# Retention offsets on GpSimd, and the outputs of a state space moved one to two steps back, split in two and spread over two PSUM banks

## The chip, the cores and the metric

The kernel runs on one core of one Trainium2 chip. The metric is the device time of one execution in microseconds (us), the median over several runs. Engines are named as the profile names them: PE is TensorE (matmuls; PEld is its weight loads), DVE is VectorE, ACT is ScalarE, POOL is GpSimd, SP is SyncE, which issues DMAs.

## The reference

A trunk of two layers runs over two groups of 1024 tokens of width 1024, each with its own conditioning vector. Layer 0 projects the normed tokens once and feeds two branches with the result: bidirectional retention with four heads of 128, and a state-space model (S5) with 32 groups of 16 channels and 64 complex states. Both are gated, concatenated and projected back. Layer 1 is neighbourhood attention. Cut to what the change touches:

```python
def _retention(q, k, v):            # chunks of 128 tokens, n = 8 chunks, 4 heads
    s = jnp.einsum('bnihd,bnjhd->bnhij', qc, kc) * intra
    o = jnp.einsum('bnhij,bnjhe->bnihe', s, vc)
    ...
    o = (o + jnp.einsum('bnihd,nbhde->bnihe', qc * q_fwd, st_f)
         + jnp.einsum('bnihd,nbhde->bnihe', qc * q_bwd, st_b))

def _head_norm(o):
    mu = jnp.mean(of, axis=-1, keepdims=True)
    var = jnp.mean(jnp.square(of - mu), axis=-1, keepdims=True)
    return (of - mu) * lax.rsqrt(var + EPS)

def _s5_scan(u, ...):               # x[t] = abar * x[t-1] + bbar * u[t], then a real part
    _, _, x_re, x_im = lax.associative_scan(_cplx_combine, elems, reverse=reverse, axis=1)
    return einsum(x_re, c_re) - einsum(x_im, c_im)
```

The S5 output of both directions goes through a tanh GELU and then a gated linear unit.

## The kernel before

All large products are split in three fp32r matmuls (high by high, low by high, high by low parts, "h_hi", "h_lo", "wh", "wl"), 128x512 each. TensorE is fed in **units**: one unit is about one half of a dense block, 24 such matmuls into bank d. After each, `unit()` (L183) steps every background task once, in the order of its list, and a task emits its next few instructions there up to its `yield`. Three tasks matter in layer 0: `s5` (the state space, four units per pair of groups, 16 pairs), `mod_blocks` (the modulation of the next layer, L341, alternating between two kinds of step) and `ret_mix` (retention of one head and one token group, L969). From the end of the first loads on, TensorE's instructions stay in the order in which the program emits them (L132, L137). DVE, ACT and POOL are ordered by a scheduler, which is why a shift in the program moves instructions there too.

PSUM has eight banks. In layer 0, bank d has two buffers and a, b, c, z, y, e have one each (`pst`, L164): the first matmul into a bank waits until every reader of its last content is done, and all later TensorE instructions wait with it.

What each part of `s5` does, for a pair `pi` of groups g = 0, 1:

- `s5_begin`: POOL builds the output tables car and cai (L685 products, sum L703, difference L706) and the input table ep (L685, sum L712), through two scratch tiles ta, tb; u is loaded.
- `s5_tables`: DVE builds the rotation tables cos and sn (four L685, then L730, L733, L734), through the same scratch tiles ta, tb.
- `s5_matrices`: TensorE transposes ep into bank e ("pev", printed pse<-ident,E), ACT copies it to em (L202); TensorE makes kernel taps in bank z ("kv"), ACT and DVE copy them (kf, k0: L202, L763, L764), and DMAs put them into mt.
- `s5_states(g)`: TensorE em by u into bank z; DVE rotates (L787, L788), POOL adds (L789), DVE scans four times (L792) and rotates back (L793, L794), POOL adds (L795).
- `s5_place(g)`: ACT copies the states, shifted, into xs (L202).
- `s5_out(g)`: six matmuls into bank y (mt by u, car and cai by the states), ACT squares (L813), DVE (L814), ACT tanh (L815), DVE (L817), store. Bank y is free after L817.

`mod_blocks` uses bank e too: in one step eight products and a copy by ACT (L202), in the next a product with the selector ("p2", printed pse<-sel), which DVE reads (L371). It does so while pairs 0 to 4 run.

In `ret_mix`, `outputs` makes the product in bank b, DVE takes statistics (L1028, L1029), L206 (DVE) and L207 (POOL, a power) make the reciprocal root brs, and DVE the offset bnb = -mean * brs (L1031). A unit later `normal` lets ACT apply both (L1037) into a tile `on`, `finish` transposes it, DVE gates it in place (L1045), and a DMA stores it to oD. Each head does this twice, first for half 1, then for half 0. Region A8 of the fixed memory map holds one sd tile (scores) and one on tile.

Of the kernel before, what the change touches and what calls it, by code (L numbers as in the profile page):

```python
# [17 lines left out]
ADD, SUB, MUL = ALU.add, ALU.subtract, ALU.mult  # L18

P = 128  # L20
# [18 lines left out]
def _parts(text):  # L39
# [28 lines left out]
MAP_L0.update(_parts("A5 gsg 1024 gsg 1024 gsg 1024 gsg 1024; A10 gth 1024 gth 1024 gbo 2048"))  # L68
MAP_L0.update(
    cosT=_fulls("A0"), sinT=_fulls("A1"), kT=_fulls("A11 A12"), qT=_fulls("A13"), ga=_fulls("A14"),  # L70
# [47 lines left out]
class Trunk:  # L118
# [573 lines left out]
    def s5_begin(self, pi):  # L692

        nc, G = self.nc, self.nc.gpsimd
        pp = self.t([P, PK], "pp")
        self.load(pp, self.ppD[pi])
        (bre, bim, cre, cim), (pwr, pwi, pwn), _ = self.s5_fields(pp)
        car = self.t([P, 2, 9, 16], "car")
        cai = self.t([P, 2, 9, 16], "cai")
        ta, tb = (self.t([P, 2, 9, 16], x) for x in ("ta", "tb"))  # L700
        self.outer(G, ta, pwr, cre)
        self.outer(G, tb, pwn, cim)
        G.tensor_tensor(car, ta, tb, ADD)  # L703
        self.outer(G, ta, pwn, cre)
        self.outer(G, tb, pwr, cim)
        G.tensor_tensor(cai, ta, tb, SUB)  # L706
        ep = self.t([P, 2, 2, 8, 16], "ep")
        for r, (x, y, op) in enumerate(((bre, bim, SUB), (bim, bre, ADD))):
            ta, tb = (self.t([P, 2, 8, 16], x) for x in ("ta", "tb"))
            self.outer(G, ta, pwr[:, :, 7::-1], x)  # L710
            self.outer(G, tb, pwi[:, :, 7::-1], y)
            G.tensor_tensor(ep[:, :, r], ta, tb, op)  # L712
        u = self.t([P, 2, 2, P], "u")
        for g in range(2):
            gi = 2 * pi + g
            for s in range(2):
                self.load(u[:, g, s], self.uD[s][gi * 16:gi * 16 + 16].rearrange("i t c -> t i c"))
        return dict(pi=pi, pp=pp, car=car, cai=cai, ep=ep, u=u, x=[None, None])

    def s5_tables(self, st):  # L720

        Vv = self.nc.vector
        cF, sF, cA, sA = self.s5_fields(st["pp"])[2]
        cos = self.t([P, 2, 8, 16], "cos")
        sn = self.t([P, 2, 2, P], "sn")
        ta, tb = (self.t([P, 2, 8, 16], x) for x in ("ta", "tb"))
        fl = lambda z: z.rearrange("p g a b -> p g (a b)")
        self.outer(Vv, ta, cA, cF)
        self.outer(Vv, tb, sA, sF)
        Vv.tensor_tensor(cos, ta, tb, SUB)  # L730
        self.outer(Vv, ta, sA, cF)
        self.outer(Vv, tb, cA, sF)
        Vv.tensor_tensor(sn[:, 0], fl(ta), fl(tb), ADD)  # L733
        Vv.tensor_scalar(sn[:, 1], sn[:, 0], -1.0, None, MUL)  # L734
        st.update(cos=cos, sn=sn)
        for d in range(2):
            rows = slice(64 * d, 64 * d + 64)
            self.copy_a(self.bm[rows, :, :, 32 * d:32 * d + 16],
                        st["pp"][rows, 0:64].rearrange("p (r g i) -> p g r i", r=2, g=2))

    def s5_matrices(self, st):

        nc, Vv, pi = self.nc, self.nc.vector, st["pi"]
        pev = self.pst("e").rearrange("p (g r x) -> p g r x", g=2, r=2)
        for g in range(2):
            for r in range(2):
                self.tr(pev[:, g, r], st["ep"][:, g, r].rearrange("p t i -> p (t i)"), self.ident)
        em = self.t([P, 2, 2, P], "em")
        self.copy_a(em, pev)
        kv = self.pst("z")[:, 0:144]  # L750
        for r, c in enumerate(("car", "cai")):
            for g in range(2):
                self.mm(kv[64 * g:64 * g + 48], self.bm[:, g, r], st[c][:, g].rearrange("p m i -> p (m i)"),
                        start=(r == 0), stop=(r == 1))
        kf = self.t([16, 2, 240], "kf")
        dd = self.t([16, 2, 16], "dd")
        k0 = self.ring(self.sml, [16, 2, 16], "k0")
        self.load(dd, self.I["dd"][:, 2 * pi:2 * pi + 2])
        for g in range(2):
            self.copy_a(kf[:, g, 0:128], kv[64 * g + 32:64 * g + 48, 16:144])  # L760
            self.copy_a(kf[:, g, 128:240], kv[64 * g:64 * g + 16, 16:128])
            self.copy_a(k0[:, g], kv[64 * g:64 * g + 16, 0:16])
        Vv.tensor_tensor(k0, k0, dd, ADD)  # L763
        Vv.tensor_tensor(kf[:, :, 112:128], k0, kf[:, :, 112:128], ADD)  # L764
        mt = self.t([P, 2, P], "mt")
        for s in range(8):
            self.load(mt[16 * s:16 * s + 16], kf[:, :, (7 - s) * 16:(7 - s) * 16 + 128])
        st.update(em=em, mt=mt)
# [34 lines left out]

    def s5_out(self, st, g):
        nc, Vv = self.nc, self.nc.vector
        x, gi = self.xs[g], 2 * st["pi"] + g
        ys = self.pst("y")[:, 0:256]
        yv = ys.rearrange("p (s c) -> p s c", s=2)
        self.mm(yv, st["mt"][:, g], st["u"][:, g], start=True, stop=False)
        self.mm(yv, st["car"][:, g, 1:9].rearrange("p m i -> p (m i)"), x[:, 0:2], start=False, stop=False)  # L810
        self.mm(yv, st["cai"][:, g, 1:9].rearrange("p m i -> p (m i)"), x[:, 2:4], start=False, stop=True)
        y2 = self.t([P, 256], "y2")
        nc.scalar.activation(y2, ys, AF.Square, scale=0.044715 ** 0.5)  # L813
        Vv.scalar_tensor_tensor(y2, y2, 1.0, ys, ADD, MUL)  # L814
        nc.scalar.activation(y2, y2, AF.Tanh, scale=G0)  # L815
        g2 = self.t([P, 2, P], "g2")
        Vv.scalar_tensor_tensor(g2.rearrange("p s c -> p (s c)"), y2, 1.0, ys, ADD, MUL)  # L817
        for s in range(2):
            self.store(self.yD[s][gi * 16:gi * 16 + 16].rearrange("i t c -> t i c"), g2[:, s])

    def s5(self, tables):

        for o, z in tables:
            self.store(self.ppD.rearrange("a p x -> p a x")[:, :, o:o + z.shape[2]], z)
        self.xs = [self.t([P, 4, P], f"xs{i}") for i in range(2)]
        self.bm = self.t([P, 2, 2, 48], "bm")
        for x in self.xs + [self.bm]:
            self.nc.gpsimd.memset(x, 0.0)
        yield
        st = self.s5_begin(0)  # L830
        yield
        self.s5_tables(st)
        yield
        self.s5_matrices(st)
        yield
        for pi in range(16):
            self.s5_states(st, 0)
            if pi:
                self.s5_out(last, 1)
            nx = self.s5_begin(pi + 1) if pi < 15 else None  # L840
            yield
            self.s5_states(st, 1)
            yield
            self.s5_place(st, 0)
            if nx:
                self.s5_tables(nx)
            yield
            self.s5_place(st, 1)
            if nx:
                self.s5_matrices(nx)  # L850
            self.s5_out(st, 0)
            last, st = st, nx
            yield
        self.s5_out(last, 1)

    def ub(self, s):
        def item(m):
# [111 lines left out]
    def ret_mix(self, s, h, r):  # L969

        nc = self.nc
# [41 lines left out]
        def outputs(j, m, bank):  # L1013
            qf, qb, sd = m
            po3 = self.pst(bank).rearrange("p (c e) -> p c e", c=4)
            for c in range(4):
                ch = 4 * j + c
                f, b = ch > 0, ch < 7
                self.mm(po3[:, c], sd[:, c], vn(ch), start=True, stop=False)
                if f:  # L1020
                    self.mm(po3[:, c], qf[:, c], stf[:, ch], start=False, stop=not b)
                if b:
                    self.mm(po3[:, c], qb[:, c], stb[:, ch], start=False, stop=True)
            st = self.ring(self.sml, [P, 4, 6], "bst")
            mv = self.ring(self.sml, [P, 4, 2], "bmv")
            rs, nb = (self.ring(self.sml, [P, 4], x) for x in ("brs", "bnb"))
            for c in range(4):
                Vv.bn_stats(st[:, c], po3[:, c])  # L1028
                Vv.bn_aggr(mv[:, c], st[:, c])  # L1029
            self.rsqrt(rs, mv[:, :, 1], 4, 1.0, EPS)  # L1030
            Vv.scalar_tensor_tensor(nb, mv[:, :, 0], -1.0, rs, MUL, MUL)  # L1031
            return po3, rs, nb

        def normal(po3, rs, nb):
            on = self.t([P, 4, P], "on")
            for c in range(4):
                nc.scalar.activation(on[:, c], po3[:, c], AF.Identity, bias=nb[:, c:c + 1], scale=rs[:, c:c + 1])  # L1037
            return on
# [513 lines left out]
```

## Time and profile before

| what | value |
|---|---|
| time, median of 3 runs | 2241.8 us (2239.88 to 2252.94) |
| the profiled execution's own time | 2248.46 us |
| its span | 2246.5 us |
| mean granted TensorE clock | 0.989 of full speed |
| PE busy | 2176.6 us, 97% of the span |
| DVE, ACT, POOL busy | 1315.4, 957.3, 746.6 us |
| chain that ended last: PE, DVE, DMA, POOL, ACT | 82%, 6%, 4%, 3%, 2% |

A busy engine is only a limit where the others wait for it. TensorE is busy nearly throughout; its few idle stretches, what ended them, and the stretches at a lower granted clock are what can be won or lost. In rows of the timeline the first two numbers are start and duration in us; x4 counts instructions shown in one row; a bracket at the end gives the idle time of the engine ahead of the instruction and what ended it.

### The profile page before, as it was taken

The page shows a single profiled execution, that of the slowest core. Times are in us where ns is not written, and L with a number is a line of the kernel's source. Part 1 is how long each engine was busy: PE and PEld are TensorE (multiplying, and loading weights), DVE is VectorE, ACT ScalarE, POOL GpSimd, SP SyncE. Part 2 cuts the span into 40 slices and gives each one's busy share as a digit, 9 for nine tenths or more (in the row PEclk, how much of TensorE's full clock was granted, in tenths as well). Part 3 has the DMA queues.
Part 4 walks back from the last instruction along what each step waited for, and adds up shares of the span by engine and source line. Part 5 has one row for each costly group of instructions (what it writes and reads, how often), then busy time and mean ns, then how long its engine had stood idle before and what let it go on. Part 6 is the DMA issues. An engine that isn't in the chain of part 4 may idle for free.

```text
span 2246.5 us, 35103 instructions
## 1 busy us (share of the span) xinstructions
PE 2176.6 (97%) x13248; PEld 1832.5 (82%) x13248; DVE 1315.4 (59%) x2885; ACT 957.3 (43%) x2098; POOL 746.6 (33%) x640
## 2 busy tenths in 40 slices
PE   6899999998999999999999999999999999999998
PEld 4667778886877888888889898888888898987886
DVE  4935768788787556566434545456555555557322
ACT  4533434435444444343334444446444444345211
POOL 2344446457465121366621111113111212113333
PEclk9999999999999999999999999999999999999999
DMA  9894222224211335534531112125111111115454
GB/s 327 264 267 127 78 83 52 67 72 129 65 58 47 95 127 178 180 132 163 166 80 44 51 46 64 46 57 111 55 50 49 51 55 55 55 38 160 113 137 125
DMA packets 296480, 231.12 MB, mean 103 GB/s; under 512 B 58488, under 2 KB 267768, under 8 KB 296312
## 3 DMA queue, kind: packets, MB, share of 16 engines
q1 hardware_dynamic: 292856, 220.51, 33.2%
q10 hardware_dynamic: 3456, 8.39, 1.1%
q8 instruction: 104, 1.70, 0.3%
q14 instruction: 64, 0.52, 0.1%
HBM read 169.92 MB, written 56.84 MB: 101 GB/s over the span
## 4 chain that ended last, share of the span: by engine, by line
PE 82%; DVE 6%; DMA 4%; POOL 3%; ACT 2%; issue 2%; SPq 0%; ACTq 0%; DVEq 0%; POOLq 0%
PE psd L131 61%; PE psc L131 5%; PE psa L131 5%; PE psb L136 4%; PE psz L131 2%; PE psy L131 2%; PE psb L131 2%; DVE E L792 1%; DMA oD<-A 1%; PE psa L136 1%; DMA wr<-in_w_in_ab 1%; PE pse L131 1%; DMA wm<-in_w_mod 0%; DMA wr<-in_w_out_ab 0%; PE psc L136 0%
## 5 line engine op out<-in xcount | busy, mean ns | idle before, releaser
L131 PE MATMUL psd<-h_hi,wh 128*128 128x512 f32 x1392 | 555.2, 399 | 8.1 <-DVE A L876 5.4
L131 PE MATMUL psd<-h_lo,wh 128*128 128x512 f32 x1392 | 547.6, 393 | 3.2 <-POOL h_lo L476 3.1
L131 PE MATMUL psd<-h_hi,wl 128*128 128x512 f32 x1392 | 545.6, 392 | 0.0
L131 PEld LDWEIGHTS psd<-h_hi,wh 128*128 128x128 f32 x1392 | 263.4, 189 | 65.2 <-DVE A L876 5.8
L131 PEld LDWEIGHTS psd<-h_lo,wh 128*128 128x128 f32 x1392 | 263.3, 189 | 58.1 <-POOL h_lo L476 5.2
L131 PEld LDWEIGHTS psd<-h_hi,wl 128*128 128x128 f32 x1392 | 263.0, 189 | 56.0 <-issue 0.4
L131 PE MATMUL psd<-wh,h_hi 128*128 128x256 f32 (+1 forms) x960 | 279.8, 304 | 3.7 <-DVE A L943 2.7
L131 PE MATMUL psd<-wl,h_hi 128*128 128x256 f32 (+1 forms) x864 | 251.7, 291 | 0.1
L202 ACT ACTIVATE wh<-wr 128x1024 fp32r<-128x1024 f32 x118 | 124.8, 1058 | 241.7 <-PE psd L131 137.0
L213 POOL TENSOR_TENSOR wl<-wr,wh 128x1024 fp32r<-128x1024 f32 x51 | 126.5, 2480 | 264.1 <-ACT wh L202 230.4
L131 PE MATMUL psd<-wh,h_lo 128*128 128x256 f32 x768 | 214.2, 279 | 0.0
L131 PEld LDWEIGHTS psd<-wh,h_hi 128*128 128x128 f32 x960 | 181.4, 189 | 12.7 <-DVE A L943 3.1
L131 PEld LDWEIGHTS psd<-wl,h_hi 128*128 128x128 f32 x864 | 163.2, 189 | 3.9 <-POOL wl L213 0.5
L131 PEld LDWEIGHTS psd<-wh,h_lo 128*128 128x128 f32 x768 | 145.4, 189 | 0.3
L1233 POOL TENSOR_TENSOR A<-A,A 128x256 f32<-128x256 f32 (+1 forms) x80 | 56.5, 727 | 264.5 <-DVE nm L1251 260.1
L213 DVE TENSOR_TENSOR wl<-wr,wh 128x1024 fp32r<-128x1024 f32 x67 | 89.5, 1336 | 72.8 <-ACT wh L202 72.8
L1253 ACT ACTIVATE E<-E,nm 128x368 f32<-128x368 f32 (+1 forms) x172 | 98.0, 571 | 52.8 <-DVE nm L1251 52.5
L395 DVE TENSOR_TENSOR rs<-ss 128x1 f32<-128x1 f32 x64 | 41.2, 643 | 119.0 <-ACT h_lo L1150 56.4
L1271 DVE COPY A<-psb 128x384 f32<-128x384 f32 x64 | 33.5, 523 | 122.6 <-PE psb L136 121.3
L685 POOL TENSOR_TENSOR A<-A 128x288 f32<-128x288 f32 (+1 forms) x128 | 93.7, 752 | 31.1 <-DVE E L733 19.5
L131 PE MATMUL psd<-ow,oh 128*128 128x512 f32 x320 | 100.4, 392 | 1.0 <-ACT oh L202 1.0
L1233 POOL TENSOR_TENSOR A<-A 128x368 f32<-128x368 f32 x16 | 13.9, 892 | 254.2 <-DVE nm L1251 253.7
(352 smaller groups left out, 4405.0 us busy)
## 6 DMA issues: line engine op xcount, KB each, us to landing
wr<-in_w_in_c SPq DMA_DIRECT2D x64, 512.0 KB
wr<-in_w_in_ab SPq DMA_DIRECT2D x48, 512.0 KB
wr<-oD SPq DMA_DIRECT2D x32, 512.0 KB
wn<-in_w_mod SPq DMA_DIRECT2D x24, 512.0 KB
wm<-in_w_mod SPq DMA_DIRECT2D x8, 1024.0 KB
ox<-in_x SPq DMA_DIRECT2D x16, 512.0 KB
x1D<-ox SPq DMA_DIRECT2D x16, 512.0 KB
oD<-E SPq DMA_DIRECT2D x32, 256.0 KB
```

Of the source, the lines that this page charges most:

```text
L131: i = self.nc.tensor.matmul(*a, **k)
L136: i = self.nc.tensor.transpose(*a, **k)
L202: self.nc.scalar.activation(dst, src, AF.Copy, scale=scale)
L213: e.tensor_tensor(lo, raw, hi.bitcast(F32), SUB)
L395: self.nc.vector.tensor_tensor(rs, ss[:, 0:1], ss[:, 1:2], ADD)
L685: eng.tensor_tensor(dst, x.unsqueeze(3).to_broadcast(sh), y.unsqueeze(2).to_broadcast(sh), op)
L792: Vv.tensor_tensor_scan(t1[:, q], r8, t1[:, q], 0.0, MUL, ADD)
L1233: self.nc.gpsimd.tensor_tensor(b, raw[a][:, c0:c0 + n], mask, ADD)
L1253: nc.scalar.activation(sn, sn, AF.Exp, bias=nm, scale=-1.0, accum_out=su)
L1271: self.nc.vector.tensor_copy(pt, pp)
```

## The change

1. In `outputs`, DVE writes bnb = -mean straight after the statistics, and after the power POOL multiplies it by brs (16 places). Before, DVE did both in one instruction after the power.
2. The `on` tile is gone: `normal` writes over the sd tile that the scores came in, and region A8 holds two sd tiles in turn.
3. In `s5` the pieces stand in other units. Per pair, units 1 to 4:

| unit | before | after |
|---|---|---|
| 1 | states(st,0); out(last,1); begin(next) | place(last,1); states(st,0); out(last,0) |
| 2 | states(st,1) | states(st,1); gelu(last,0); out(last,1); begin(next) |
| 3 | place(st,0); tables(next) | gelu(last,1); tables(next) |
| 4 | place(st,1); matrices(next); out(st,0) | place(st,0); matrices(next) |

`s5_out` is cut in two: matmuls, square and L814 stay; tanh and the rest are `s5_gelu`. Output 0 goes into bank y, output 1 into bank e. The two copies into bm move from the tables to the matrices.

```diff
-    "A7 qf 2048 qb 2048; A8 sd 2048 on 2048; A9 vfb 2048 th 2048; A10 rt1 2048 rt2 2048")
+    "A7 qf 2048 qb 2048; A8 sd 2048 sd 2048; A9 vfb 2048 th 2048; A10 rt1 2048 rt2 2048")
...
     def s5_out(self, st, g):
         nc, Vv = self.nc, self.nc.vector
-        x, gi = self.xs[g], 2 * st["pi"] + g
-        ys = self.pst("y")[:, 0:256]
+        x = self.xs[g]
+        ys = self.pst("ye"[g])[:, 0:256]
...
         nc.scalar.activation(y2, ys, AF.Square, scale=0.044715 ** 0.5)
         Vv.scalar_tensor_tensor(y2, y2, 1.0, ys, ADD, MUL)
+        st["y"][g] = ys, y2
+
+    def s5_gelu(self, st, g):
+        nc, Vv, gi = self.nc, self.nc.vector, 2 * st["pi"] + g
+        ys, y2 = st["y"][g]
         nc.scalar.activation(y2, y2, AF.Tanh, scale=G0)
...
+        last = None
         for pi in range(16):
+            if last:
+                self.s5_place(last, 1)
             self.s5_states(st, 0)
-            if pi:
+            if last:
+                self.s5_out(last, 0)
+            yield
+            self.s5_states(st, 1)
+            if last:
+                self.s5_gelu(last, 0)
                 self.s5_out(last, 1)
             nx = self.s5_begin(pi + 1) if pi < 15 else None
             yield
-            self.s5_states(st, 1)
+            if last:
+                self.s5_gelu(last, 1)
+            if nx:
+                self.s5_tables(nx)
             yield
             self.s5_place(st, 0)
             if nx:
-                self.s5_tables(nx)
-            yield
-            self.s5_place(st, 1)
-            if nx:
                 self.s5_matrices(nx)
-            self.s5_out(st, 0)
             last, st = st, nx
             yield
-        self.s5_out(last, 1)
+        self.s5_place(last, 1)
+        for g in range(2):
+            self.s5_out(last, g)
+            yield
+            self.s5_gelu(last, g)
...
+            Vv.tensor_scalar(nb, mv[:, :, 0], -1.0, None, MUL)
             self.rsqrt(rs, mv[:, :, 1], 4, 1.0, EPS)
-            Vv.scalar_tensor_tensor(nb, mv[:, :, 0], -1.0, rs, MUL, MUL)
-            return po3, rs, nb
-
-        def normal(po3, rs, nb):
-            on = self.t([P, 4, P], "on")
+            G.tensor_tensor(nb, nb, rs, MUL)
+            return po3, rs, nb, sd
+
+        def normal(po3, rs, nb, on):
```

In the lines of the changed kernel all numbers behind the changed loop are 15 higher (L1037 is L1052, L943 is L958, L876 is L891); tanh is L820, the last DVE step of an output L822, and POOL's new multiply L1047.

**TensorE, unit 2 of pair 2.** psz<-E are the states of group 1, pse<-sel is p2 of `mod_blocks`. Before:

```order
L131 MATMUL psd_2313<-h_hi,wl_1755 128x512
L131 MATMUL psz_2346<-E_193_1408 64x256 [waits DMAHW4_49,DMAHW5_49,DVE_49,PE_49]
L131 MATMUL psz_2346<-E_193_1408 64x256 x3
L131 MATMUL pse_2361<-sel,A_191_1393 128x2 [waits Activation_49]
L131 MATMUL psb_2365<-vn_237_1809,A_257_2084 128x128
```

After:

```order
L131 MATMUL psd_2282<-h_hi,wl_1751 128x512
L131 MATMUL psz_2315<-E_193_1408 64x256 [waits DMAHW5_49,DMAHW6_49,DVE_49,PE_49]
L131 MATMUL psz_2315<-E_193_1408 64x256 x3
L131 MATMUL pse_2334<-E_193_1408,E_198_1452 128x256 [waits Activation_49]
L131 MATMUL pse_2334<-E_183_1343,A_192_1395 128x256
L131 MATMUL pse_2334<-E_183_1343,A_184_1344 128x256
L131 MATMUL pse_2357<-sel,A_191_1393 128x2 [waits DVE_49,PE_49]
L131 MATMUL psb_2361<-vn_236_1797,A_257_2080 128x128
```

The six matmuls of output 1 (three rows, each for two parts) now stand in bank e directly ahead of p2, which goes into bank e as well and now waits for DVE. The same stands in units 2 of pairs 1, 3 and 4.

**DVE, the same unit.** L787, L788 rotate the states, L213 makes a low weight part, L876 or L891 the gate of retention, L814 and L822 belong to output 1, L792 are the scans, L371 reads p2. Before:

```order
L787 TENSOR_TENSOR E_217_1593<-psz_2346,E_198_1452 128x512
L788 TENSOR_TENSOR E_217_1593<-psz_2346,E_183_1343 128x512
L371 TENSOR_TENSOR mods<-pse_2361,bmod 128x2
L213 TENSOR_TENSOR wl_2340<-wr_2338,wh_2339 128x1024
L876 SCALAR_TENSOR_TENSOR ga_2243<-A_259_2093,psd_2313 128x512
```

After:

```order
L787 TENSOR_TENSOR E_217_1593<-psz_2315,E_198_1452 128x512
L788 TENSOR_TENSOR E_217_1593<-psz_2315,E_183_1343 128x512
L213 TENSOR_TENSOR wl_2309<-wr_2307,wh_2308 128x1024
L891 SCALAR_TENSOR_TENSOR ga_2231<-A_259_2089,psd_2282 128x512
L814 SCALAR_TENSOR_TENSOR A_184_1344<-A_184_1344,pse_2334 128x256
L792 SCALAR_TENSOR_TENSOR E_217_1593<-A_191_1393,E_217_1593 128x128 x4
L822 SCALAR_TENSOR_TENSOR E_198_1452<-A_184_1344,pse_2334 128x256
L793 TENSOR_TENSOR E_217_1593<-E_217_1593,E_183_1343 128x512
L371 TENSOR_TENSOR mods<-pse_2357,bmod 128x2
```

L822, the last reader of bank e, stands behind L213, the gate, L814 and the four scans. In pair 1 it stands directly behind L814; in pair 3 behind L213, L958, L959, L814, four L792 and L960; in pair 4 behind L958, L959, L814 and L960.

**POOL, units 2 to 4 of pair 2, after the change.** L712 are the two sums of ep, L795 the last step of the states, L1019 and L1020 belong to retention:

```order
L795 TENSOR_TENSOR E_217_1593<-E_217_1593 128x512
L712 TENSOR_TENSOR E_183_1343<-A_191_1393,A_192_1395 128x2x128
L1020 TENSOR_TENSOR A_256_2079<-qT_1699,A_210_1540 128x512
L685 TENSOR_TENSOR A_191_1393<-A_191_1393 128x256
L685 TENSOR_TENSOR A_192_1395<-A_191_1393 128x256
L1019 TENSOR_TENSOR A_256_2079<-qT_1699,A_210_1540 128x512
L207 TENSOR_TENSOR brs_2375<-brs_2375,mhalf 128x4
L712 TENSOR_TENSOR E_183_1343<-A_191_1393,A_192_1395 128x2x128
L1047 TENSOR_TENSOR bnb_2376<-bnb_2376,brs_2375 128x4
```

The second L712, on which pev waits, stands behind L795; before the change both L712 stood ahead of the L795 of group 1.

## Rows read from the trace of the kernel before

**Rows 1.** The page, part 1: busy time of each engine.
```profile
PE 2176.6 (97%) x13248; PEld 1832.5 (82%) x13248; DVE 1315.4 (59%) x2885; ACT 957.3 (43%) x2098; POOL 746.6 (33%) x640
```

**Rows 2.** Windows: length, busy of PE, PEld, DVE, ACT, POOL, then PEclk.
```profile
250.00:850.00 600.00, 569.88 (x3310) 475.93 (x3309) 441.42 (x861) 258.94 (x565) 295.76 (x273) 0.97 0.28 81
```

**Rows 3.** Waits of PE, 230 to 830 us: total, times, longest.
```profile
PE psy L131 <- DVE E L817: 6.4, 4, 2.8
PE psa L131 <- DVE qT L945: 5.9, 2, 3.5
PE psd L131 <- DVE A L876: 5.4, 1, 5.4
PE psz L131 <- ACT k L202: 3.9, 3, 2.3
PE pse L131 <- ACT E L202: 2.9, 1, 2.9
PE psd L131 <- DVE A L943: 2.7, 1, 2.7
```

**Rows 4.** Windows that begin at the end of four of these waits.
```profile
280.00:287.00 7.00, 7.00 (x33) 6.82 (x34) 3.49 (x12) 2.25 (x10) 0.00 (x0) 0.57 0.41 122
312.00:316.00 4.00, 3.83 (x16) 3.23 (x17) 4.00 (x8) 1.30 (x4) 3.90 (x3) 0.66 0.55 167
371.00:375.00 4.00, 3.11 (x10) 2.50 (x11) 1.62 (x3) 1.80 (x6) 0.91 (x2) 0.57 0.09 21
531.00:538.00 7.00, 6.53 (x21) 5.24 (x22) 6.44 (x12) 3.11 (x4) 2.27 (x3) 0.70 0.75 218
```

**Rows 5.** Timeline: two outputs, from their matmuls to DVE's last step.
```profile
215.39 1.03 PE L131 MATMUL psy<-E,A 128*128 128x256 f32 x4
...
217.78 0.42 DVE L817 SCALAR_TENSOR_TENSOR E<-A,psy 128x256 f32<-128x256 f32 x1 [0.48 <-ACT A L815]
...
332.02 0.70 PE L131 MATMUL psy<-E,E 128*128 128x256 f32 x2
...
332.56 1.03 PE L131 MATMUL psy<-E,A 128*128 128x256 f32 x4
...
336.25 3.92 DVE L792 TENSOR_TENSOR_SCAN E<-A,E 128x128 f32<-128x128 f32 x4
340.08 0.39 DVE L817 SCALAR_TENSOR_TENSOR E<-A,psy 128x256 f32<-128x256 f32 x1
```

**Rows 6.** DVE by line and shape, 230 to 830 us: busy, mean ns.
```profile
L792 DVE TENSOR_TENSOR_SCAN E<-A,E 128x128 f32<-128x128 f32 x115 | 74.1, 703 | 11.9 <-POOL E L789 11.9
L685 DVE TENSOR_TENSOR A<-A 128x256 f32<-128x256 f32 x54 | 37.7, 736 | 6.9 <-POOL E L712 6.7
L213 DVE TENSOR_TENSOR wl<-wr,wh 128x1024 fp32r<-128x1024 f32 x25 | 35.5, 1422 | 18.1 <-ACT wh L202 18.1
L944 DVE TENSOR_TENSOR A<-A,sinT 128x512 f32<-128x512 f32 x28 | 24.1, 860 | 0.0
...
L943 DVE TENSOR_TENSOR A<-psd,cosT 128x512 f32<-128x512 f32 x28 | 19.2, 685 | 8.7 <-ACT A L202 8.6
...
L945 DVE TENSOR_TENSOR kT<-A 128x512 f32<-128x512 f32 x14 | 11.7, 837 | 0.1
```

**Rows 7.** Timeline near 565 us: POOL's sum of ep and of states, pev.
```profile
563.85 0.74 POOL L712 TENSOR_TENSOR E<-A,A 128x256 f32<-128x256 f32 x1
...
567.39 0.60 PE L136 MATMUL pse<-ident,E 128*128 128x128 f32 x4
...
570.06 1.50 POOL L795 TENSOR_TENSOR E<-E 128x512 f32<-128x512 f32 x1 [2.97 <-DVE E L794]
```

**Rows 8.** Chain of waits, 350 to 375 us: the store of half 1.
```profile
356.13 7.86 DMA oD<-A
```

**Rows 9.** Lines L1031 and L207: instructions, shortest, median, longest ns.
```profile
L1031 DVE SCALAR_TENSOR_TENSOR bnb<-bmv,brs x16: 149/164/2330, 275.4 to 848.1; 128x4 f32<-128x4 f32 x16
...
L207 POOL TENSOR_TENSOR brs<-brs,mhalf x16: 1007/1018/1461, 272.3 to 846.8; 128x4 f32<-128x4 f32 x16
```

More of the change, by code (lines that the diff above doesn't have):

```diff
@@ L717, in s5_begin @@
                 self.load(u[:, g, s], self.uD[s][gi * 16:gi * 16 + 16].rearrange("i t c -> t i c"))
-        return dict(pi=pi, pp=pp, car=car, cai=cai, ep=ep, u=u, x=[None, None])
+        return dict(pi=pi, pp=pp, car=car, cai=cai, ep=ep, u=u, x=[None, None], y=[None, None])
     def s5_tables(self, st):
@@ L735, in s5_tables, with s5_matrices @@
         st.update(cos=cos, sn=sn)
+    def s5_matrices(self, st):
+        nc, Vv, pi = self.nc, self.nc.vector, st["pi"]
         for d in range(2):
@@ L739, in s5_tables @@
                         st["pp"][rows, 0:64].rearrange("p (r g i) -> p g r i", r=2, g=2))
-    def s5_matrices(self, st):
-        nc, Vv, pi = self.nc, self.nc.vector, st["pi"]
         pev = self.pst("e").rearrange("p (g r x) -> p g r x", g=2, r=2)
```

## The prediction

> **What bounds the kernel now.** I read the busy times first: TensorE works through 97% of the span and no other engine through more than 59% [rows 1], so a piece of work moved off DVE, ACT or POOL is worth nothing by itself. Only what makes TensorE wait, or run at the lower clock, can be won or lost. So I looked next at the stretch that the change touches, 250 to 850 us. There TensorE is idle for 600 - 569.88 = 30.1 us, and the mean granted clock is 0.97, which is 0.03 * 600 = 18 us of lost clock [rows 2]. Together 48 us, 2.1% of the time: more than that no reordering of this stretch can give.
>
> Then the table of TensorE's waits, to see who ends the 30 us. The reader is to see six entries: bank y waits for the last DVE step of an output (6.4 us, four times), the scores of retention for the rotary step (5.9), bank z for ACT's copies of the taps (3.9), p2 in bank e for ACT's copy of em (2.9), one dense half for DVE's rotary step (2.7) and one for the gate (5.4) [rows 3]. Last, the clock behind these waits. Four windows that begin where a wait ends show it at 0.57, 0.66, 0.57 and 0.70, part of the window at the half level of 1.2 GHz [rows 4]. (1 - 0.57) * 7 = 3.0 us, 0.34 * 4 = 1.4, 0.43 * 4 = 1.7 and 0.30 * 7 = 2.1 us are lost there: 2.0 us on the mean. A wait of 2 us or more so costs nearly twice its length.
>
> **What can be won.** Bank y took two outputs per pair, close behind each other; it takes one now, with four units between them, so the 6.4 us of bank y go. The copies of the taps are late for two reasons: an output stood behind them in the same unit, which is moved, and once `normal` waited for the store of half 1, 7.86 us long [rows 8], which the second sd tile ends; the 3.9 us go. The tables move behind the states of group 1 and mostly behind the rotary steps on DVE; four L685 of 0.736 us are 2.9 us of DVE that the rotary step no longer waits for [rows 6], which covers 5.9 us in two places and 2.7 in one to the greater part. I take 6.4 + 5.9 + 3.9 + 2.7 = 18.9 us. Five of these waits (those near 312, 371, 572, 668 and 726 us) are 2 us or longer; with 1.55 us each, the mean of the second and third window of rows 4, the clock gives 7.8 us. The 2.9 us in front of p2 come from a chain on ACT that begins with the offsets of retention; after the change the offset stands on POOL behind one L712, so it comes hardly earlier. I count half of 2.9 + 3.0 us, 3.0. The 5.4 us behind the gate hang on a load of weights and activations that the change leaves where it is: nothing. **Gain 18.9 + 7.8 + 3.0 = 29.7 us** (bounds: 15 if half of the waits only move; 40 with all of p2 and the gate's 5.4 + 2.1).
>
> **What it costs: bank e.** In units 2 of pairs 1 to 4 the output into bank e stands directly ahead of p2 in the same bank, and p2 must now wait for DVE's L822. There is no work between them that would cover it, and all dense work is queued behind p2. The trace gives the time from the end of an output's matmuls to the end of its last DVE step: 215.39 + 1.03 = 216.42 to 218.20, so 1.8 us with DVE free, and 333.59 to 340.47, so 6.9 us with scans between [rows 5]. Which it is, DVE's order decides; L787 and L788, two steps of about 0.69 us, fit beside the 1.6 us of the matmuls themselves. Pair 1: nothing between, 1.8 us. Pair 2: 1.42 (L213) + 0.69 (gate, priced as L943) + 0.41 + 4 * 0.70 (scans) + 0.41 = 5.7. Pair 3: 1.42 + 0.69 + 0.86 + 0.41 + 2.81 + 0.84 + 0.41 = 7.4. Pair 4: 0.69 + 0.86 + 0.41 + 0.84 + 0.41 = 3.2 [rows 5, 6]. That is 18.1 us (bounds 4 * 1.8 = 7.1 and 4 * 7.4 = 29.7). Behind each the clock falls: 4 * 2.0 = 8.0 (0, if waits of 1.8 us leave it alone, to 4 * 3.0 = 12). **26.1 us.**
>
> The Trainium skill bears on this (TensorE: Matmul & The Clock Gate, section "A second HAM failure mode: psum-queue depth-cycling"): a kernel that cycled through its PSUM banks left TensorE idle for short times between its groups so often that the clock kept falling and rising, although each matmul looked no longer at full clock. The windows behind the waits agree with that, 0.57 to 0.70 [rows 4]; by the rule alone the shortest of the four waits would pay as the others do, 8.0 us as in the sum, and the short waits that go would have given more.
>
> **The em copy.** In unit 4 the six matmuls of an output, 332.02 to 333.59 or 1.6 us [rows 5], stood between the transposes of ep and p2, while ACT copied em out of the same bank. They are gone, so p2 waits sooner at its four places: between 0 and 4 * 1.6 = 6.3 us. **I take 3.**
>
> **pev.** POOL's second L712 stands behind L795 now. Near 565 us L795 ended at 571.56; with 0.74 for L712 the transposes could start at 572.3, against 567.39 before, 4.9 us later [rows 7]. But the 2.9 us of L685 and the waits of the tables for POOL leave the way ahead of these states, so about 2 remain, and at most pairs pev comes later in the unit. I take 3 us of idle in all and one fall of 1.6, **5 us** (bounds 0, and five pairs at 4.9 + 1.6 = 32).
>
> **The rest, at nothing.** POOL's multiply of 128x4 has no row of its own: between DVE's 0.16 us for the same numbers and the power's 1.02 [rows 9]; it is nearest to the power, one POOL instruction of the same shape, so 1.0, sixteen times. It replaces a wait of bnb in DVE's queue, and `normal` follows a unit later, which hides it; without that cover it would delay ACT and the transposes behind it by 1 us, 16 in all. The additional DVE step costs the 0.16 that the old one did. The pieces moved to other units take ACT, DVE and their stores with them in equal numbers; ACT is busy for 258.94 of 600 us [rows 2], and that hides them. The last two outputs end up to two units later, ahead of the gated linear unit; if the retention work does not cover that, it is one wait of at most 6.9 us.
>
> On the multiply the Trainium skill speaks against the change (GPSIMD Engine Reference, section "Engine selection"): elementwise work with two inputs belongs on VectorE, since GpSimd takes about twice as long. No row here shows this very product on both engines; by the page it would be about 0.3 us, an estimate, and at either figure the sum stays.
>
> **Sum.** Cost 26.1 + 3 + 5 = 34.1, gain 29.7, net +4.4 on the profiled execution's 2248.46, so 2252.9. That execution lies 6.7 us above the median of the runs, 2241.8; so **2246 us**.
>
> **The rivals.**
> *Short waits on bank e.* DVE reaches L822 at all four places as fast as it did at 217.78 [rows 5]: 7.1 us and no fall of the clock, 19 less than in the sum: 2227. For it speaks that TensorE, once held, lets DVE catch up; against it, that the order puts the scans and the rotary steps ahead of L822. If the gate's wait went too (7.5), it would be 2220.
> *pev waits for POOL*, the one that ends slower. If L794 comes no earlier, five of the pairs wait 4.9 us at the transposes and pay 1.6 for the clock: 32.5 in place of 5: 2246 + 27.5 = 2274. It decides from the point where L712 ends more than 3 us behind the last dense matmul of unit 3 in most pairs. For it: the chain L794, L795, L712 is serial and stands at 571.56 + 0.74 against 567.39 [rows 7]. Against: the tables' DVE work leaves its front.
> *Stalls only move.* Half of the gain comes back elsewhere, since DVE has the same work (441 of 600 us) [rows 2]: 2246 + 15 = 2261.
>
> **How the numbers follow.** I give my forecast (2232 to 2260) 0.52, the short waits 0.16, the POOL wait 0.18, the moved stalls 0.14. About 1% (22 us) is what a measurement of this kernel tells from no change: faster means below 2219, slower above 2264. Below 2219 needs the short waits and more: 0.09. Above 2264 lie nearly all of the POOL wait and a part of the moved stalls: 0.24. The rest, 0.67, is within 1%. The range from 2226 (short waits) to 2272 (just under the full POOL wait) leaves out about 0.07 below and 0.12 above.
>
> **What would show it.** In the waits of the changed kernel: the entries of bank y and of k gone; a new one, bank e for DVE's L822, four times, some 18 us, beginning in units 2 of pairs 1 to 4, with a clock near 0.6 behind each; the scores without a wait for the rotary step; the gate's 5.4 us still there. If bank e totals under 9 us, the term for DVE's order is wrong; if bank e waits for POOL's L712 by more than 8 us, the term for pev is. If the waits for the rotary step or for k remain, the gain was overrated, and the prediction fails on the slow side.

## The result and the profile after

The changed kernel takes 2262.2 us (median of 4 runs, 2260.5 to 2266.6), the kernel before 2242.9 on the same occasions (2239.9 to 2252.9). The ratio is 1.0085, 95% interval 1.0070 to 1.0099: 19 us slower, 0.85%. Forecast were 2246 us and a range of 2226 to 2272. The time lies in the range, 2 us above the 2232 to 2260 that stood for the forecast's own account and 2 us below the 2264 from which the prediction would call it slower. The sign of the sum was right (+4.4), its size was not.

TensorE's waits in the changed kernel, 200 to 870 us; the columns are those of [rows 3]:

```profile
PE pse L131 <- DVE E L822: 23.8, 4, 7.8
PE pse L136 <- POOL E L712: 16.5, 9, 6.1
PE pse L131 <- ACT E L202: 4.4, 4, 1.7
```

Five of the six entries of [rows 3] are gone. The sixth, p2 behind the em copy, has grown from 2.9 us in one place to 4.4 in four. Two new entries stand beside it, of bank e like it: p2 behind the output of group 1, and the transposes of ep behind POOL's second sum. The stretch as a whole, first of the kernel before, then of the changed one (columns as in [rows 2]):

```profile
200.00:870.00 670.00, 639.67 (x3809) 537.09 (x3808) 486.90 (x949) 293.19 (x646) 314.96 (x295) 0.97 0.28 82
```

```profile
200.00:870.00 670.00, 625.35 (x3685) 523.29 (x3684) 453.89 (x925) 287.46 (x631) 309.80 (x309) 0.95 0.27 78
```

TensorE is idle for 670 - 625.35 = 44.7 us where it was 30.3. That is 14.3 of the 18.4 us by which the profiled span grew (2264.9 us against 2246.5). The rest, some 4 us, is put down to the clock, whose mean falls from 0.97 to 0.95. Where the idle time lies, from the timeline of TensorE in the changed kernel:

```profile
203.22 0.38 PE L131 MATMUL pse<-sel,A 128*128 128x2 f32 x2 [1.70 <-ACT E L202]
...
223.35 0.35 PE L131 MATMUL pse<-sel,A 128*128 128x2 f32 x2 [1.92 <-DVE E L822]
...
266.13 0.56 PE L131 MATMUL pse<-sel,A 128*128 128x2 f32 x2 [6.41 <-DVE E L822]
...
286.94 0.38 PE L131 MATMUL pse<-sel,A 128*128 128x2 f32 x2 [1.70 <-ACT E L202]
...
317.23 0.56 PE L131 MATMUL pse<-sel,A 128*128 128x2 f32 x2 [7.79 <-DVE E L822]
...
365.46 0.56 PE L131 MATMUL pse<-sel,A 128*128 128x2 f32 x2 [7.64 <-DVE E L822]
...
558.51 0.90 PE L136 MATMUL pse<-ident,E 128*128 128x128 f32 x3 [6.08 <-POOL E L712]
...
593.92 0.90 PE L136 MATMUL pse<-ident,E 128*128 128x128 f32 x3 [4.12 <-POOL E L712]
```

The four waits of p2 for L822 are those of units 2 of pairs 1 to 4. The clock behind the first, the third and the largest wait for POOL, in windows that begin where the wait ends or within a microsecond of it:

```profile
224.00:228.00 4.00, 4.00 (x23) 3.82 (x23) 4.00 (x9) 0.00 (x0) 2.66 (x4) 0.63 0.26 69
317.00:323.00 6.00, 5.78 (x19) 4.96 (x20) 5.01 (x8) 1.82 (x5) 6.00 (x6) 0.54 0.25 82
558.00:564.00 6.00, 5.49 (x19) 4.01 (x20) 5.48 (x3) 5.38 (x13) 5.42 (x5) 0.50 0.36 117
```

PEclk is 0.63, 0.54 and 0.50, though TensorE is busy through nearly all of each window: it works at 1.2 GHz, the lower of its two levels, for most of it. Even the 1.92 us in front of the first p2 are paid for that way. Not every short wait is: behind the two waits of 1.70 us for the em copy, at 203 and 287 us, the clock is full in one case and not in the other.

```profile
203.00:207.00 4.00, 3.77 (x33) 3.78 (x34) 2.28 (x8) 1.75 (x9) 1.70 (x2) 1.00 0.50 138
287.00:291.00 4.00, 4.00 (x25) 4.00 (x26) 2.22 (x7) 1.49 (x8) 0.00 (x0) 0.68 0.64 198
```

With what the Trainium skill says in the place cited in the prediction (TensorE: Matmul & The Clock Gate, "A second HAM failure mode: psum-queue depth-cycling") the trace agrees in part: the clock fell behind short waits at a change of bank, 0.50 to 0.68, but not behind the one at 203 us.

### The profile page after: what moved, and what is told of

It reads as the page before. It is cut to its first block, busy times and chain, and to the rows that moved or that the text cites. A ratio compares the mean times of both kernels' runs of the same rounds, so it can differ in the third digit from the quotient of the medians.

```text
span 2264.9 us, 35115 instructions
## 1 busy us (share of the span) xinstructions
PE 2180.0 (96%) x13248; PEld 1836.0 (81%) x13248; DVE 1295.2 (57%) x2885; ACT 958.6 (42%) x2098; POOL 743.0 (33%) x656
## 4 chain that ended last, share of the span: by engine, by line
PE 80%; DVE 6%; DMA 6%; POOL 4%; ACT 2%; issue 2%; SPq 1%; ACTq 0%; DVEq 0%; POOLq 0%
PE psd L131 59%; PE psc L131 5%; PE psa L131 4%; PE psb L136 4%; DMA out_y<-h_lo 3%; PE psz L131 2%; PE psb L131 2%; DVE E L792 2%; PE pse L131 1%; PE psy L131 1%; POOL A L685 1%; POOL E L795 1%; SPq L191 1%; PE psa L136 1%; POOL E L712 1%
## 5 line engine op out<-in xcount | busy, mean ns | idle before, releaser
L213 POOL TENSOR_TENSOR wl<-wr,wh 128x1024 fp32r<-128x1024 f32 x51 | 126.5, 2480 | 269.9 <-ACT wh L202 265.2
L213 DVE TENSOR_TENSOR wl<-wr,wh 128x1024 fp32r<-128x1024 f32 x67 | 88.6, 1324 | 80.0 <-ACT wh L202 79.8
L685 POOL TENSOR_TENSOR A<-A 128x288 f32<-128x288 f32 (+1 forms) x128 | 94.8, 761 | 49.7 <-DVE E L733 39.0
L1248 POOL TENSOR_TENSOR A<-A 128x368 f32<-128x368 f32 x16 | 13.9, 890 | 254.3 <-DVE nm L1266 253.7
```

What stands on the lines that cost most here:

```text
L213: e.tensor_tensor(lo, raw, hi.bitcast(F32), SUB)
L685: eng.tensor_tensor(dst, x.unsqueeze(3).to_broadcast(sh), y.unsqueeze(2).to_broadcast(sh), op)
L1248: self.nc.gpsimd.tensor_tensor(b, raw[a][:, c0:c0 + n], mask, ADD)
```

## The experiments

The kernel before ran beside every set of runs; its median was between 2242.9 and 2250.1 us by occasion, so kernels are compared by their ratio to it. A hundredth is about 22 us. All kernels lie within 2% of the one before; where two intervals overlap, their order is not shown.

| kernel | ratio to before | 95% interval |
|---|---|---|
| the change | 1.0085 | 1.0070 to 1.0099 |
| p2 in bank y | 0.9953 | 0.9938 to 0.9968 |
| ep made first | 1.0047 | 1.0031 to 1.0063 |
| both of these | 0.9904 | 0.9883 to 0.9925 |
| both, offset back on DVE | 0.9930 | 0.9915 to 0.9944 |
| both, tables in unit 4 | 0.9926 | 0.9911 to 0.9940 |
| both outputs in bank y | 0.9966 | 0.9951 to 0.9981 |
| both outputs in bank y, ep first | 0.9961 | 0.9946 to 0.9975 |
| only the state space | 1.0097 | 1.0080 to 1.0114 |
| only the retention parts | 0.9968 | 0.9955 to 0.9981 |
| only the second sd tile | 0.9977 | 0.9964 to 0.9990 |
| only the offset on POOL | 0.9956 | 0.9942 to 0.9970 |

**Is it bank e?** The theory was that p2 waits since it shares a bank with the output ahead of it; the rival, that DVE is the limit here and the wait would turn up elsewhere.

```diff
-            p2 = self.pst("e")[:, 0:2]
+            p2 = self.pst("y")[:, 0:2]
```

> The changed kernel, but p2 of the modulation goes into bank y instead of bank e, so that it no longer follows the output of group 1 into the same bank; everything else stays. Theory (bank e): the four waits for L822, 23.8 us, and about 2 us of lost clock behind each leave, 2262 - 32 = about 2230, at most a third of it given back as longer waits for POOL at the transposes: 2228 to 2242. Rival (DVE is the limit in this stretch and the waits only move): TensorE waits for DVE at the rotary or gate steps instead, idle time in all stays near 44 us, 2252 to 2264.

Measured: 2234.6 us, ratio 0.9953, as the theory said. One letter is worth 0.0132, some 30 us, and turns the loss into a gain. The waits of TensorE, 200 to 870 us:

```profile
PE pse L136 <- POOL E L712: 21.9, 12, 6.5
PE pse L131 <- issue: 1.4, 1, 1.4
```

The entry of L822 is gone, and so is that of the em copy: in unit 4, p2 no longer shares the bank that ACT reads. What comes back is 5.4 us of waiting for POOL. Idle time falls from 44.7 to 23.3 us (646.66 us busy of 670), by 21.3; the profiled span shrinks by 28.6 us, and the 7 us between the two are put down to the clock. The rival falls: DVE has the same work and keeps up.

**Is it POOL's second sum?** Theory: the transposes wait since ep is made too late. Rival: POOL is late as a whole.

```diff
             if last:
                 self.s5_out(last, 0)
+            nx = self.s5_begin(pi + 1) if pi < 15 else None
             yield
...
-            nx = self.s5_begin(pi + 1) if pi < 15 else None
+            if nx:
+                self.s5_rest(nx)
             yield
```

`s5_begin` keeps the load of the parameters and ep; car, cai and the load of u move from it into `s5_rest`.

> The changed kernel, but the table ep (both sums of POOL) is made in unit 1, a unit before car, cai and the load of u; bank e stays as changed. Theory (POOL's second sum stands behind the states of group 1): the 16.5 us at the transposes and some 7 us of clock leave, 2262 - 23 = about 2239 (2234 to 2248), the four waits for L822 stay at 18 to 26 us. Rival (POOL as a whole is late): the wait moves one row on, to the taps (bank z) which need car and cai, and the time stays at 2256 to 2266.

Measured: 2254.5 us, ratio 1.0047; 0.0038 or 8.5 us better than the change, where 23 were expected. The waits of TensorE:

```profile
PE pse L131 <- DVE E L828: 22.6, 4, 7.6
PE psd L131 <- DVE A L967: 6.3, 1, 6.3
...
PE psd L131 <- DVE A L900: 4.2, 2, 3.5
PE psz L131 <- ACT k L202: 4.1, 1, 4.1
```

POOL's 16.5 us are gone, but 14.6 us come back, 13.9 of them in three places, each 5 to 11 us behind transposes that had waited for POOL (by 6.1, 4.1 and 2.1 us) before: a dense half waits for DVE's rotary step (L967, which is L958 of the change) or gate (L900), bank z for the copies of the taps. So neither theory nor rival held as told. The transposes did wait for POOL, but DVE and ACT were late there too, and the wait for POOL had covered part of that.

**Both together.** p2 in bank y and ep first.

> The changed kernel with both mends: p2 in bank y, and ep made a unit ahead of car, cai and u. Theory (two independent losses, the second backed by DVE's own lateness at pairs 10, 11 and 15): bank e and POOL's sum leave the waits; of the 21.9 us at the transposes some 14 come back as waits for DVE's gate and rotary steps and for the copies of the taps, as in the kernel with ep first: 2234.6 - 8 to 12 = 2222 to 2228. Rival (the two mends give the same time twice): 2232 to 2238.

Measured: 2229.8 us, ratio 0.9904: 1.0% faster than before and 1.8% faster than the change, the lowest ratio of all, though its interval overlaps those of its two variants below. The time lies between theory and rival; the ratio, taken where the kernel before needed 2250.0 us and not 2244.5, speaks for the theory: the gains add up within their intervals (0.0132 + 0.0038 = 0.0170 against 0.0181), as two independent losses would. Of the 21.9 us at the transposes 17.6 come back, where 14 were expected:

```profile
PE psz L131 <- ACT k L202: 8.7, 2, 4.5
PE psd L131 <- DVE A L967: 4.9, 1, 4.9
PE psd L131 <- DVE A L900: 4.0, 2, 3.5
```

**Does an output need a second bank?** The changed kernel with both outputs in bank y, first with ep as changed, then with ep first; p2 stays in bank e.

```diff
-        ys = self.pst("ye"[g])[:, 0:256]
+        ys = self.pst("y")[:, 0:256]
```

> The changed kernel with both outputs in bank y, at the changed places; p2 stays in bank e. Theory (what costs is that bank e is shared with p2, not that outputs move): the second output waits for L822 of the first, which stands a unit earlier and is mostly done, under 6 us in all; the four waits of p2 go: 2230 to 2240, as with p2 in bank y. Rival (an output needs a bank of its own): the wait moves to bank y, four or more times 4 us, 2245 to 2262.

Measured: 2243.6 us beside 2250.0 of the kernel before, ratio 0.9966; by the ratio the theory holds. The wait for L822 goes as with p2 in bank y, and bank y has no entry in the waits; the gain over the change is 0.0119. Most of the loss came not from moving the outputs but from where the second one was put; POOL's sum remains (21.5 us). With ep first:

> The changed kernel with both outputs in bank y and ep made first; p2 stays in bank e. Theory (the second bank brings nothing; bank e only has to be left to p2): no wait for bank y above 1 us, ratio to before 0.989 to 0.993, as with both mends. Rival (the short waits of p2 for ACT's em copy, 2.7 us, and a new one of bank y cost more): 0.994 to 0.998.

Measured: ratio 0.9961, as the rival said. The waits:

```profile
PE psz L131 <- ACT k L202: 8.8, 2, 4.6
PE pse L131 <- ACT E L202: 6.5, 4, 3.0
...
PE psy L131 <- DVE E L828: 3.0, 2, 2.0
```

Once POOL's wait no longer holds TensorE up, bank y waits again (3.0 us), and p2 for the em copy in full (6.5 us). The kernel with both mends is faster by 0.0057, but it differs in two things, the bank of output 1 and that of p2. Of the waits named here the larger part is p2's, so what a second bank for the outputs is worth by itself is not shown.

**The retention parts, alone and left out.**

> The kernel before with only the retention parts of the change: the offset on POOL and the second sd tile in place of on. Theory: the wait of ACT for the store of half 1 near 364 us goes, with it up to 4.3 us of idle TensorE and 1.7 of clock: 2243 - 6 = 2237 (2232 to 2242). Rival (the store's wait was covered or another takes its place): 2243 within 2. The multiply on POOL is expected at 0.6 to 1.1 us.

Measured: 2237.5 us, ratio 0.9968, 7 us faster than before, as the theory said; whether by the store is the question below.

> The changed kernel without the retention parts: offset on DVE after the power, on tile back; the moved and split outputs stay. Theory (all of the loss is in the state space): 2262 to 2268, bank e again 18 to 26 us and POOL's sum 12 to 20. Rival (the additional POOL instruction, which stands among POOL's work for ep, makes the transposes late): POOL's sum under 8 us and 2250 to 2256.

Measured: ratio 1.0097; its waits are those of the change (bank e 23.6 us, POOL's sum 16.2). All of the loss is in the state space, and the retention parts soften it by 0.0012, which their intervals do not tell apart from nothing. Which of the two parts gains:

> The kernel before with the second sd tile in place of on, offset still on DVE. Theory (the store of half 1 is what held ACT near 364 us): nearly all of the gain of the retention parts, 2236 to 2241. Rival (the offset does it): 2242 to 2246.

Measured: 2243.8 us beside 2250.0, ratio 0.9977 or 5 us; by the ratio the theory holds. ACT's wait for the store near 364 us is gone, but ACT then waits 1.0 us for the offset there, and TensorE's 2.3 us behind it [rows 3] only shrink to 0.8.

> The kernel before with the offset of retention on POOL, on tile kept. Theory (the offset is covered by the unit between statistics and normal): within 2 us of before, 2242 to 2246, the multiply at 0.2 us. Rival (it frees ACT earlier everywhere): 2235 to 2240.

Measured: 2240.6 us beside 2250.0, ratio 0.9956, 10 us faster than before: the rival. The multiply takes 0.2 us, the price was not the point. Alone the two parts gain 0.0023 and 0.0044, together only 0.0032, so the gains do not add up, and how they share it is not shown. There is a wait on DVE that I had not read. The kernel before has, among the waits of DVE from 200 to 870 us:

```profile
DVE bnb L1031 <- POOL brs L207: 16.2, 13, 3.5
```

In 13 places DVE's queue stood still for the power on POOL, up to 3.5 us, and gates, rotary steps and low weight parts stood behind it. With the offset on POOL the entry is gone; of the waits of TensorE in that kernel:

```profile
PE psy L131 <- DVE E L817: 9.4, 5, 3.3
...
PE psd L131 <- DVE A L943: 0.9, 1, 0.9
PE psd L131 <- DVE A L876: 0.8, 1, 0.8
```

Against [rows 3] the gate's 5.4 us are down to 0.8 and the rotary step's 2.7 to 0.9, both steps of DVE, while bank y's 6.4 are up to 9.4. That the standing queue of DVE is what cost the 10 us is argued and not shown. The changed kernel without the retention parts speaks against it: DVE waits there as long,

```profile
DVE bnb L1046 <- POOL brs L207: 18.9, 12, 3.5
```

and TensorE's waits are still those of the change, with none for the gate. Does the offset matter with both mends?

```diff
-            Vv.tensor_scalar(nb, mv[:, :, 0], -1.0, None, MUL)
             self.rsqrt(rs, mv[:, :, 1], 4, 1.0, EPS)
-            G.tensor_tensor(nb, nb, rs, MUL)
+            Vv.scalar_tensor_tensor(nb, mv[:, :, 0], -1.0, rs, MUL, MUL)
```

> The kernel with both mends (p2 in bank y, ep first), but the offset of retention back on DVE behind the power. Theory (the offset on DVE holds DVE's queue while POOL computes the power, 16 us of idle DVE in 13 places in the kernel before): the wait comes back on DVE at 8 to 20 us, and the ratio to before goes from 0.990 to 0.993 - 0.997. Rival (the offset was covered, as the prediction said): 0.989 to 0.991.

Measured: ratio 0.9930. DVE's wait comes back:

```profile
DVE bnb L1055 <- POOL brs L207: 19.5, 13, 3.5
```

But the interval overlaps that of both mends (0.9883 to 0.9925), and TensorE's waits are the same within 0.6 us in every entry, though DVE stands for 19.5 us. Not decided: what the offset is worth here is between nothing and 12 us.

**A try at the rest.** Both mends, and the tables in unit 4 behind the statistics of retention.

```diff
             if last:
                 self.s5_gelu(last, 1)
-            if nx:
-                self.s5_tables(nx)
             yield
             self.s5_place(st, 0)
             if nx:
+                self.s5_tables(nx)
                 self.s5_matrices(nx)
```

> The kernel with both mends, and the tables moved from unit 3 to unit 4, behind the statistics of retention in DVE's queue. Theory (the offset comes late since the tables stand ahead of the statistics on DVE, ACT waits for it near 355 and 701 us and the taps' copies with it): the two waits of bank z for k, 8.7 us, go or shrink below 4, and the dense half's 4.9 us for the rotary step near 560 goes: ratio 0.984 to 0.988. Rival (the tables then delay the states of the next unit 1): new waits at the transposes or at bank z, 0.990 to 0.998.

Measured: ratio 0.9926. The waits for k (8.8 us) and for the rotary step (5.1) stand as before. The theory falls: the tables are not what makes them late. The time lies in the rival's range, but the new waits that it names do not appear. ACT sits behind `normal` and its offset near 355 us, as in the kernel with both mends; what makes the offset late there stays open.

## Why the prediction came out as it did

**What bounds the kernel: right.** Only TensorE's idle time and clock moved. 14.3 us of idle time and, by difference, some 4 of clock are the 18.4 us between the two profiles. One reading was too high: the four waits ahead of the windows of [rows 4] are 2.9, 2.5, 4.3 (two in a row) and 5.4 us long, 15.1 in all, and 8.2 us of clock were lost behind them. That is half their length, so such a wait costs one and a half times its length and not nearly twice; the sum, which took 2.0 us per wait, does not change.

**The gain: right in kind, too small by the gate.** All four entries that the sum counts as gone went. The gate's 5.4 us went too, which I had counted as staying because it hung "on a load of weights and activations that the change leaves where it is". The reading was right, the conclusion was not. ACT, then DVE, in the kernel before:

```profile
525.47 1.06 ACT L202 ACTIVATE h_hi<-hraw 128x1024 fp32r<-128x1024 f32 x1 [5.42 <-DMA hraw<-hD]
526.44 1.04 ACT L202 ACTIVATE wh<-wr 128x1024 fp32r<-128x1024 f32 x1
```

```profile
527.51 3.31 DVE L213 TENSOR_TENSOR wl<-wr,wh 128x1024 fp32r<-128x1024 f32 x1 [1.42 <-ACT wh L202]
530.74 0.67 DVE L876 SCALAR_TENSOR_TENSOR A<-A,psd 128x512 f32<-128x512 f32 x1
```

A weight part stands on ACT behind the instruction that waits for the load, and the gate on DVE behind that weight part. With only the offset on POOL, ACT makes a weight part first and then waits 1.39 us for the load, and the gate's wait is 0.8 us. With only the second sd tile it is 3.0 us, and in the changed kernel without the retention parts it is gone. So the load can stay where it is and the wait can still go, by the order in front of it; which part of the change did it stays open.

**The offset, priced at nothing: wrong for the kernel before, open for the change.** I looked at the new instruction (taken as 1.0 us, it takes 0.2) and at its reader, and not at the wait that the old one held on DVE. Alone, in the kernel before, it is worth 0.0044. In the changed kernel both retention parts together are worth 0.0012 and with both mends the offset 0.0026, and neither is told apart from nothing. The multiply in the changed kernel, shortest, median and longest:

```profile
L1047 POOL TENSOR_TENSOR bnb<-bnb,brs x16: 201/202/648, 276.2 to 863.1; 128x4 f32<-128x4 f32 x16
```

The estimate of 0.3 us by the Trainium skill (GPSIMD Engine Reference, "Engine selection") was nearer than the nearest row, the power of the same shape: that one computes something else.

**Bank e: the mechanism right, the term mis-sized.** 18.1 us were worked out, 23.8 measured. By pairs 1.8, 5.7, 7.4 and 3.2 were said, 1.9, 6.4, 7.8 and 7.6 it is. Three of four places follow from DVE's order alone. Pair 4 does not, since adding up durations leaves out what the instructions wait for themselves. DVE in the changed kernel there:

```profile
356.98 0.68 DVE L788 TENSOR_TENSOR E<-psz,E 128x512 f32<-128x512 f32 x1
361.59 0.69 DVE L958 TENSOR_TENSOR A<-psd,cosT 128x512 f32<-128x512 f32 x1 [3.92 <-ACT A L202]
...
364.91 0.41 DVE L822 SCALAR_TENSOR_TENSOR E<-A,pse 128x256 f32<-128x256 f32 x1
```

and ACT, whose copy (the last row) is what L958 waits for:

```profile
356.40 1.26 ACT L202 ACTIVATE E<-E 64x508 f32<-64x508 f32 x2 [7.27 <-POOL E L795]
...
360.35 1.21 ACT L202 ACTIVATE A<-psd 64x512 f32<-64x512 f32 x2
```

ACT waits 7.27 us for POOL's L795, then copies states, does `normal` (1.50 us) and a weight part (1.06 us) and only then the copy; DVE's queue stands for 3.92 us, and TensorE at p2 with it. The clock term, 8.0 us, is near the 7 us by which p2 in bank y gave back more than idle time.

**The em copy.** The prediction takes half of the 2.9 us away and adds 3, which makes 4.4 us; 4.4 it is. Both halves were guesses between bounds, so this is luck; in the kernel with both outputs in bank y and ep first it is 6.5.

**pev: the term that failed.** I took 3 us of idle time, 16.5 came. The rival that I had put at 0.18 names this place and mechanism; it expected five pairs at 4.9 us, and there were two at 4.1 and 6.1 and seven short ones. The step that failed is the sentence that priced what follows L795 with one L712, 0.74 us. POOL in the changed kernel, near 555 and near 590 us:

```profile
553.33 2.18 POOL L795 TENSOR_TENSOR E<-E 128x512 f32<-128x512 f32 x1 [1.82 <-DVE E L794]
555.47 2.18 POOL L685 TENSOR_TENSOR A<-A 128x256 f32<-128x256 f32 x2
557.73 0.73 POOL L712 TENSOR_TENSOR E<-A,A 128x256 f32<-128x256 f32 x1
...
586.69 1.28 POOL L795 TENSOR_TENSOR E<-E 128x512 f32<-128x512 f32 x1 [1.35 <-DVE E L794]
587.93 1.19 POOL L712 TENSOR_TENSOR E<-A,A 128x256 f32<-128x256 f32 x1
589.08 2.83 POOL L213 TENSOR_TENSOR wl<-wr,wh 128x1024 fp32r<-128x1024 f32 x1
591.88 1.19 POOL L685 TENSOR_TENSOR A<-A 128x256 f32<-128x256 f32 x2
593.15 0.72 POOL L712 TENSOR_TENSOR E<-A,A 128x256 f32<-128x256 f32 x1
```

Both products of the second sum stand behind L795 as well, as the order shown ahead of the prediction has them, and near 590 us the first sum and a weight part too. From the end of L795 to the end of the second L712 it is 2.9 us in the first place and 5.9 in the second, not 0.74. The rest of the longest wait is that the states were late: TensorE stood from 552.4 us on, and L795 ended at 555.5. So the DVE work taken out of their way did not make up for it there.

**The sum.** In idle time the prediction had costs of 22.6 us (18.1 at bank e, 3 at pev and, for the em copy, 3 less the 1.5 that it counts as gain) against 18.9 of gain. Measured, the costs are 23.8 + 16.5 and 1.3 more for the em copy (4.4 against 3.1 in this window), 41.6 us, and the gain is 27.1: the five entries, 24.3, and a wait at the end of the gated linear unit which the prediction did not count, in the kernel before:

```profile
PE psz L131 <- ACT A L930: 2.8, 1, 2.8
```

The costs were too low by 5.7 us at bank e and 13.5 at pev, the gain by 5.4 at the gate and 2.8 here. The result is the small difference of two larger sums, which is why an error in either could make one as large as the result. That the time still lies in the range is in part luck, since the two errors offset each other. It also lies beside the 2261 us of the rival by which stalls only move, but the waits do not bear that rival out: five entries left, and with p2 in bank y the kernel is faster than before.

## What to carry to other kernels

Before a matmul is put into a bank that has one buffer, list every later matmul into that bank, up to the first by which its readers are sure to be done; one short matmul too early, as p2 here, holds all that is queued behind it. Price the wait by following the reader's queue with its own waits, not by adding durations, and price a chain on another engine with all instructions that the printed order shows in it. Where an instruction leaves an engine, look also at what that engine waited for in front of it, here 16 us of DVE in 13 places, and then test whether anything critical stood behind that wait: moving the offset gained 10 us in one kernel and nothing that could be told apart from noise in another.

## What the runs showed of the hardware

DVE is slower beside POOL by more than I had expected. An L685 of DVE, 0.736 us on the mean [rows 6], took over three times as long while POOL worked on two large low parts, and half of that mean right after them. DVE, then POOL, in the changed kernel:

```profile
558.49 5.12 DVE L685 TENSOR_TENSOR A<-A 128x256 f32<-128x256 f32 x2 [1.90 <-POOL E L712]
...
564.11 0.76 DVE L685 TENSOR_TENSOR A<-A 128x256 f32<-128x256 f32 x2
```

```profile
558.41 2.36 POOL L453 TENSOR_TENSOR h_lo<-hraw,h_hi 128x1024 fp32r<-128x1024 f32 x1
560.73 2.60 POOL L213 TENSOR_TENSOR wl<-wr,wh 128x1024 fp32r<-128x1024 f32 x1
```

Two of them took 5.12 us, about as long as POOL was busy with these two; the next two, with POOL idle, took 0.76. The Trainium skill (GPSIMD Engine Reference, "Key points") says that GpSimd shares its interfaces to SBUF with VectorE and that DVE instructions with two SBUF inputs contend for them; the rows agree, but no run here was made to take one of the two away, so the cause is argued and not shown.
